# A hybrid decoder layer in fp32: head 3 projected by stored weight units, and the last head's output rows ahead of its decays

## The chip, the cores and the metric

The kernel is one program on **one core** of a Trainium2 chip. The metric is the device time of one execution in microseconds; three executions of the kernel before took 2317.92, 2318.16 and 2319.36 us, median **2318.16 us**. The engines of the core are called by their names in the profile: PE (TensorE: matrix products; PEld is its loading of weights), DVE (VectorE), ACT (ScalarE), POOL (GpSimd) and SP (SyncE, which here issues nearly all transfers).

## The reference

One decoder layer on x of 1024 tokens x 1024 features, all in float32:

```python
x = x + 0.5 * swiglu(rms_norm(x, ffn1_norm), w_gate1, w_up1, w_down1)      # d_ff = 2816
x = x + hybrid_mixer(rms_norm(x, mix_norm), w_in, ..., w_out)
x = x + 0.5 * swiglu(rms_norm(x, ffn2_norm), w_gate2, w_up2, w_down2)
return rms_norm(x, final_norm)

def hybrid_mixer(h, ...):
    proj = h @ w_in            # q, k, v, z of 8 GDN heads x 128; gates b, a; z, x, B, C, dt of 16 SSM heads x 64
    q, k, v = silu(causal_dwconv(gdn_qkv, gdn_conv_w))
    o = gated_delta_rule(q, k, v, g, beta)                                  # chunked: a triangular solve per chunk
    o_gdn = rms_norm(o, gdn_norm_w) * silu(gdn_z)
    y = ssd_scan(...)          # Mamba-2, then gated by silu(ssm_z), rms_norm in two groups
    return concat([o_gdn, o_ssm]) @ w_out
```

The gated delta rule of one head: with the decays g and the step sizes beta, the products k kᵀ of each block give a lower triangular system; its inverse is applied to v and k, and a state of 128 x 128 is carried through the 8 blocks of 128 tokens.

## The kernel before, in words

**Products.** Every float32 operand of a large product is split into a rounded part (hi) and the rest (lo); ScalarE makes hi by a cast (L241) and VectorE lo by a subtraction (L242). TensorE then runs three products, hi·hi, hi·lo and lo·hi (`mm3`, L121 to L125). The two feed-forward parts and part of the projection into the mixer use Strassen's scheme, 7 products of half-sized operands in place of 8. In the gate and up phase these are L334 to L336; after each product a hook `prep` prepares operands of a coming one. ScalarE's SiLU of the gate is L380, its read-outs of PSUM are L343.

**Weight units.** The mixer projects q, k, v and z of its 8 GDN heads from the same normed tokens. `NESTED` is the number of heads (0, 1, 2, 3) that are projected directly, by `proj_half`: 2 column pairs x 2 columns x 2 halves x 8 blocks x 3 products. Heads 4 to 7 go by Strassen in two *chunks* each (chunk 2i holds k and q of a head, chunk 2i + 1 v and z). A chunk has 7 *units*: a combination of blocks of W_in, split into hi and lo. The units are made long before they are used, in the first feed-forward part, by the generator `win_units`: each `next` of it makes one unit, by one or two casts (tile `wunit`), at times a sum or difference (tile `wsum`) and two stores to `wu_scr` in DRAM. The raw columns (`wraw`) are loaded at the start of a chunk. `UP_CHUNKS` = 6 chunks are made in the gate and up phase, driven by `prep` in each step i, and the other 2 in the down phase, driven by `Down.prep`, which is called once for each block of w_down. In the mixer `chunk` loads a chunk's units back (4 slots), and L1259 to L1261 multiply them with token combinations.

**A GDN head.** For each of its 8 heads the mixer's loop
- loads the cumulated decays and takes two exponentials (`qe`, L1361, and `dt`, L1364, with a triangular mask on GpSimd between them);
- projects and convolves q, k, v and gates z (`qt`, `kt`, `vt_`, `zc`);
- runs the key part `k_part`: 8 transposes of `kt` (L1345), their squares' sums (`jd`, L1349) and the decayed keys `kd` (L1350);
- forms the products k kᵀ and k qᵀ (L1426, L1427), and solves the triangular systems: a substitution of 31 steps on VectorE (L1476, L1478), an exchange through DRAM (`fs_x`), then small products on TensorE (from L1496 on);
- carries the state through 8 blocks, norms the result (`sso`, `co`, `vr`, L1567) and stores it to `mix_scr`.

The solve and the state chain of a head run while TensorE does the projection of the next head. The last head (7) has no next one; in its place stand the first output rows: `out_start` loads 256 rows of W_out (x) and the scanned SSM output (y), makes w (hi, lo) and mtt (hi by L1200, lo by L1201), and `group_tile(0, …)` forms the first 4 row blocks x 2 halves of the output (`FIRST_TILES`), read out of PSUM by L1220 into `xa`. `group_prep(1)` does the same for the next 256 rows.

**Order.** Each engine takes its instructions in its own fixed order. A scheduler sets it when the program is built, from the order of the code, the free buffers and pins (`tc.issue_after`). The code of the last head before:

```python
copy = chunk(pre[:, 3:3 + L], zc)                 # L1397: the units of v and z
    A.activation(out=kt, in_=kt, func=AF.Silu)    # L1399
tk, br2, kd = k_part(h, kt)                       # L1400
    A.activation(out=qt, in_=qt, func=AF.Silu)    # L1402
if h == GH - 1:
    out_start()                                   # L1404
conv_from(pre, 16 + h, vt_)
A.activation(out=zc, in_=zc, func=AF.Silu)
A.activation(out=vt_, in_=vt_, func=AF.Silu)
```

with `group_prep(1)` and the 8 calls of `group_tile(0, …)` behind it, and the two exponentials at the head of the loop.

Of the kernel before, what the change touches and what calls it, by code (L numbers as in the profile page):

```python
# [11 lines left out]
F32 = mybir.dt.float32  # L12
# [9 lines left out]
P = 128  # L22
# [22 lines left out]
def kernel(  # L45
# [28 lines left out]
    wu_scr = [dram.tile([P, 7, 2, 512], F32, name=f"wu_scr{i}") for i in range(2 * (GH - 4))]  # L74
# [279 lines left out]
    def gate_up_all(pool, H, w_gate, w_up, scr, raws, ops, last, work, tail, side):  # L354
# [66 lines left out]
        for i, (p, w) in enumerate(todo):  # L421
# [7 lines left out]
            def prep(grp):  # L429

                if nxt:
                    made = a_ops(pool, *((raws[0], m, nxt[0]) for m in A_GROUPS[grp]))
                    if i == 2 and grp == 0:
                        first_hid(made)
                    with ExitStack() as pins:
                        if i == 4 and grp == 0:
                            for e in made:
                                pins.enter_context(tc.issue_after(e.ins))
                        for _ in range(0 if i < 4 else 2 if grp and i % 3 == 1 else 1):
                            next(side, None)  # L440
                elif tail:
                    tail.pop(0)()
                if raws and grp == 1:
                    next_load()
# [57 lines left out]
    class Down:  # L502
# [25 lines left out]
        def prep(self):  # L528
            if self.cnt % 2:
                next(self.side, None)  # L530
# [109 lines left out]
    for h in range(4):  # L640
        w_seq.append((COL_Q + h * P, COL_K + h * P))
        w_seq.append((COL_V + h * P, COL_GZ + h * P))
# [11 lines left out]
    NESTED, UP_CHUNKS = 4, 6  # L654
# [556 lines left out]
    def group_tile(n, b, dh, w, m):  # L1211
        bs = slice(b * P, (b + 1) * P)
        ds = slice(dh * 512, (dh + 1) * 512)
        p = psum("pj")
        for j in range(2):
            last = mm3(p, m[0][:, j, bs], m[1][:, j, bs], w[0][:, j, ds], w[1][:, j, ds], j == 0, j == 1)
        o = out_bufs[0][b // 2][:, b % 2, ds]
        r = rstd_g[n // 2][:, b:b + 1]
        if n == 0:
            A.mul(out=o, in_=p, mul=r)  # L1220
        else:
            V.scalar_tensor_tensor(out=o, in0=p, scalar=r, in1=o, op0=ALU.mult, op1=ALU.add)
        return last

    FIRST_TILES = 4
    out_bufs, ready0 = [], []

    def out_start():
# [8 lines left out]
        for j in range(2):  # L1237
            split(w[0][:, j], w[1][:, j], x[:, j])
            ssm_split(0, j, y, *m)
# [93 lines left out]
    with ExitStack() as cg:  # L1333
        g1 = cg.enter_context(tc.tile_pool(name="gdn1", bufs=1, reuse_waits="tile"))
        g2 = cg.enter_context(tc.tile_pool(name="gdn2", bufs=2, reuse_waits="tile"))
        def k_part(h, kt):
# [4 lines left out]
            for half in range(2):  # L1341
# [4 lines left out]
                for i in range(4):  # L1346
# [3 lines left out]
                    A.mul(out=kd[:, b], in_=pt[:, i * P:(i + 1) * P], mul=wend[:, b, h:h + 1])  # L1350
# [5 lines left out]
        for h in range(GH):  # L1356
            hl = h % 2
# [5 lines left out]
            for b in range(NB):  # L1363
                A.activation(out=dt[:, b], in_=dt[:, b], func=AF.Exp, bias=ngc[:, b, h:h + 1])  # L1364
            qt = gp.tile([P, L], F32, name="qt", tag="xst", bufs=2)
            kt = g2.tile([P, L], F32, name="kt", bufs=3)
            vt_ = g1.tile([P, L], F32, name="vt_")
            if h < NESTED:
# [3 lines left out]
                tk, br2, kd = k_part(h, kt)  # L1372
# [15 lines left out]
            else:  # L1388
# [11 lines left out]
                tk, br2, kd = k_part(h, kt)  # L1400
                with tc.issue_after(copy.ins):
                    A.activation(out=qt, in_=qt, func=AF.Silu)  # L1402
                if h == GH - 1:
                    out_start()  # L1404
                conv_from(pre, 16 + h, vt_)
                A.activation(out=zc, in_=zc, func=AF.Silu)
                A.activation(out=vt_, in_=vt_, func=AF.Silu)
            nc.sync.dma_start(out=z_scr[h], in_=zc)
            if h == GH - 1:
                ready1 = group_prep(1)  # L1410
                for b in range(FIRST_TILES):
                    for dh in range(2):
                        tile_end = group_tile(0, b, dh, *ready0[0])
# [6 lines left out]
            for b0 in range(0, NB, 2):  # L1420
# [8 lines left out]
                for i in range(2):  # L1429
# [5 lines left out]
                                in1=dt[:, b2], op=ALU.mult)  # L1435
            fs_u = dram.tile([4, NB, 32, 32], F32, name="fs_u", bufs=2)
# [301 lines left out]
```

## Time and profile before

| | |
|---|---|
| median of 3 executions | 2318.16 us (2317.92 to 2319.36) |
| the profiled execution's own time | 2318.03 us |
| its span in the profile | 2316.3 us |
| mean granted clock of TensorE | 0.993 |
| instructions | 31,987 |
| read from DRAM, written | 249.34 MB, 105.52 MB |

The profile's views that are read below: the **page** has busy time of each engine and the *chain that ended last*, which follows the work back from the last instruction through what released each step. The **waits** of an engine list line, releaser, and then us in total, number and the longest. The **stretches** give for a window A:B (us from the start of the span) its length, the busy time of each engine with the number of instructions, the granted clock of TensorE (PEclk, 1.00 is full speed), the share of time in which the DMA engines moved something, and GB/s. In the **timeline** a row has the time at which the instruction starts, its duration, engine, line and operation, out<-in, the size, and in brackets a wait ahead of it; rows of the same kind that follow one another are folded (x8) with the sum of their durations. **Groups** (line, engine, operation) have busy time and mean ns of one, then the idle time ahead of them and what ended it. **Transfers** have KB each and us from issue to landing.

### The profile page before, as it was taken

What the parts mean: (1) busy time and instruction counts of PE and PEld (TensorE: products, weight loads), DVE (VectorE), ACT (ScalarE), POOL (GpSimd) and SP (SyncE); (2) the same over time, 40 slices, a digit from 0 to 9 for tenths busy, and PEclk for the clock granted to TensorE, in tenths of its full rate; (3) what the DMA queues carried; (4) which work ended last, traced back from release to release, by engine and by line L of the source; (5) the groups of instructions that cost most, each with busy time, mean ns of one, the idle gap of its engine ahead of it and who ended that gap; (6) DMA issues with size and microseconds to landing.
All of it is one profiled execution on the core that took longest, in us unless ns stands there. A gap on an engine that the chain in (4) does not pass through costs nothing.

```text
span 2316.3 us, 31987 instructions
## 1 busy us (share of the span) xinstructions
PE 2267.1 (98%) x11654; PEld 1848.9 (80%) x11654; DVE 1753.3 (76%) x3217; ACT 1179.7 (51%) x2284; POOL 50.6 (2%) x117
## 2 busy tenths in 40 slices
PE   7999999999999999999999998999999999999998
PEld 5788888888878878877877776888878888888886
DVE  8998987769777787656667778578698777766787
ACT  7444433354367985874655557432443333334344
POOL 0000000000000110000000000000000000000000
PEclk9999999999999999999999999899999999999999
DMA  3467663496653343242356556335223333329445
GB/s 111 159 210 241 228 207 115 170 334 214 210 187 125 128 128 98 69 128 65 83 165 180 168 172 216 103 98 191 91 72 119 109 106 109 104 89 357 138 154 214
DMA packets 262194, 356.96 MB, mean 154 GB/s; under 512 B 60808, under 2 KB 167404, under 8 KB 260244
## 3 DMA queue, kind: packets, MB, share of 16 engines
q1 hardware_dynamic: 261364, 352.73, 46.7%
q8 instruction: 91, 1.49, 0.3%
q0 software_dynamic: 672, 2.19, 0.2%
q14 instruction: 67, 0.55, 0.1%
HBM read 249.34 MB, written 105.52 MB: 153 GB/s over the span
## 4 chain that ended last, share of the span: by engine, by line
PE 79%; DVE 9%; ACT 7%; DMA 2%; issue 2%; POOL 0%; SPq 0%; DVEq 0%; ACTq 0%; POOLq 0%
PE ps_pj L124 6%; PE ps_pj L123 6%; PE ps_pj L125 6%; PE ps_pj L334 6%; PE ps_pj L335 6%; PE ps_pj L336 6%; PE ps_mx L334 3%; PE ps_mx L336 3%; PE ps_mx L335 3%; PE ps_pj L564 2%; PE ps_pj L565 2%; PE ps_pj L563 2%; PE ps_pj L1259 2%; PE ps_pj L1261 2%; PE ps_pj L1260 2%
## 5 line engine op out<-in xcount | busy, mean ns | idle before, releaser
L336 PE MATMUL ps_pj<-bh,al 128*128 128x512 f32 x688 | 267.9, 389 | 0.0
L335 PE MATMUL ps_pj<-bl,ah 128*128 128x512 f32 x688 | 267.8, 389 | 0.0
L334 PE MATMUL ps_pj<-bh,ah 128*128 128x512 f32 x688 | 267.5, 390 | 0.0
L125 PE MATMUL ps_pj<-hhi,wlo 128*128 128x512 f32 x576 | 229.9, 399 | 0.0
L123 PE MATMUL ps_pj<-hhi,whi 128*128 128x512 f32 x576 | 229.4, 398 | 0.4 <-ACT gsb L901 0.4
L124 PE MATMUL ps_pj<-hlo,whi 128*128 128x512 f32 x576 | 228.9, 397 | 0.0
L335 PEld LDWEIGHTS ps_pj<-bl,ah 128*128 128x128 f32 x688 | 129.2, 188 | 26.7
L336 PEld LDWEIGHTS ps_pj<-bh,al 128*128 128x128 f32 x688 | 129.2, 188 | 26.7
L334 PEld LDWEIGHTS ps_pj<-bh,ah 128*128 128x128 f32 x688 | 129.0, 188 | 26.6
L242 DVE TENSOR_TENSOR al<-as,ah 128x512 fp32r<-128x512 f32 x220 | 141.1, 685 | 7.3 <-ACT ah L241 6.8
L317 DVE TENSOR_TENSOR as<-wst 128x512 f32<-128x512 f32 x220 | 144.3, 684 | 2.5 <-DMA wst<-in_ffn_w_up_dram 2.4
L241 ACT CAST ah<-wst 128x512 fp32r<-128x512 f32 x88 | 54.5, 621 | 179.1 <-PE ps_oo L335 116.7
L241 ACT CAST hid<-hraw 128x1024 fp32r<-128x1024 f32 (+1 forms) x84 | 82.2, 980 | 123.6 <-PE ps_oo L565 45.6
L334 PE MATMUL ps_mx<-bh,ah 128*128 128x512 f32 x352 | 139.3, 398 | 5.2 <-ACT sg L380 2.1
L335 PE MATMUL ps_mx<-bl,ah 128*128 128x512 f32 x352 | 139.0, 395 | 0.4 <-DVE bl L242 0.4
L336 PE MATMUL ps_mx<-bh,al 128*128 128x512 f32 x352 | 138.2, 393 | 1.0 <-DVE al L242 1.0
L241 ACT CAST ah<-as 128x512 fp32r<-128x512 f32 x220 | 125.2, 617 | 19.6 <-DVE as L317 19.5
L123 PEld LDWEIGHTS ps_pj<-hhi,whi 128*128 128x128 f32 x576 | 108.4, 188 | 21.6 <-ACT gsb L901 0.9
L124 PEld LDWEIGHTS ps_pj<-hlo,whi 128*128 128x128 f32 x576 | 108.4, 188 | 21.4 <-issue 0.8
L125 PEld LDWEIGHTS ps_pj<-hhi,wlo 128*128 128x128 f32 x576 | 108.3, 188 | 20.9 <-issue 0.5
L242 DVE TENSOR_TENSOR hid<-hraw,hid 128x1024 fp32r<-128x1024 f32 (+1 forms) x84 | 95.0, 1131 | 26.6 <-ACT hid L241 26.3
L343 ACT COPY m<-ps_pj 128x512 f32<-128x512 f32 x88 | 51.6, 588 | 112.9 <-PE ps_pj L336 112.7
(502 smaller groups left out, 5651.6 us busy)
## 6 DMA issues: line engine op xcount, KB each, us to landing
hraw<-hid_scr SPq DMA_DIRECT2D x70, 512.0 KB, 4.3
wu_scr<-wunit SPq DMA_DIRECT2D x112, 256.0 KB, 3.2
wunits<-wu_scr SPq DMA_DIRECT2D x56, 512.0 KB, 4.7
hid_scr<-hs SPq DMA_DIRECT2D x110, 256.0 KB, 3.0
wst<-in_ffn_w_down_dram SPq DMA_DIRECT2D x50, 512.0 KB, 4.7
wst<-in_ffn_w_gate_dram SPq DMA_DIRECT2D x22, 1024.0 KB, 5.6
wst<-in_ffn_w_up_dram SPq DMA_DIRECT2D x22, 1024.0 KB, 5.5
hid_scr<-sg SPq DMA_DIRECT2D x44, 256.0 KB, 2.0
```

Source lines behind the costliest of these rows:

```text
L123: T.matmul(o, lhsT=wh, rhs=mh, start=first, stop=False)
L124: T.matmul(o, lhsT=wh, rhs=ml, start=False, stop=False)
L125: return T.matmul(o, lhsT=wl, rhs=mh, start=False, stop=last)
L241: return (A.copy(out=hi, in_=src), V.tensor_tensor(out=lo, in0=src, in1=hi.bitcast(F32), op=ALU.subtract))
L242: V.tensor_tensor(out=lo, in0=src, in1=hi.bitcast(F32), op=ALU.subtract))
L317: V.tensor_tensor(out=t, in0=v[0], in1=v[1], op=v[2])
L334: T.matmul(bank, lhsT=wh[:, k], rhs=bh[:, k], start=a, stop=False, skip_group_check=True)
L335: T.matmul(bank, lhsT=wh[:, k], rhs=bl[:, k], start=False, stop=False, skip_group_check=True)
L336: T.matmul(bank, lhsT=wl[:, k], rhs=bh[:, k], start=False, stop=z, skip_group_check=True)
L343: A.copy(out=t, in_=bank)
L563: T.matmul(bank, lhsT=hh, rhs=wh, start=first and k == 0, stop=False, skip_group_check=True)
L564: T.matmul(bank, lhsT=hh, rhs=wl, start=False, stop=False, skip_group_check=True)
```

## The change

The number of directly projected heads goes from 4 to 3 (`NESTED`), so head 3 is projected by units like heads 4 to 7. There are then 10 chunks of units instead of 8: 7 are made in the gate and up phase and 3 in the down phase. In the gate and up phase the first units still come at step i = 4; from there on each first `prep` of a step makes one unit and each second one two (before: two in every third step). In step 4 the units of both are pinned behind the operands that the `prep` makes (before: of the first alone). In the down phase three of five calls make a unit (before: every second).

In the mixer the key part of a directly projected head moves behind its z. In the last head, `out_start` makes both halves of mtt ahead of the splits of w, the 8 calls of `group_tile(0, …)` stand ahead of the key part and of the decays (now a function, `decays`), the decayed keys are made by VectorE, the convolution of v and the SiLUs of z and v come behind them, z is stored from GpSimd's queue, and `group_prep(1)` stands behind the products k kᵀ, pinned behind the sixth read-out of the output rows (`moved[5]`).

```diff
@@ -71,7 +71,7 @@
     g_scr = dram.tile([NG, L], F32, name="g_scr")
-    wu_scr = [dram.tile([P, 7, 2, 512], F32, name=f"wu_scr{i}") for i in range(2 * (GH - 4))]
+    wu_scr = [dram.tile([P, 7, 2, 512], F32, name=f"wu_scr{i}") for i in range(2 * (GH - 3))]
     t_scr = {m: dram.tile([P, 2, 4, 512], F32, name=f"t_scr{m}") for m in (4, 5, 6, 7)}
@@ -433,10 +433,10 @@
                     with ExitStack() as pins:
-                        if i == 4 and grp == 0:
+                        if i == 4:
                             for e in made:
                                 pins.enter_context(tc.issue_after(e.ins))
-                        for _ in range(0 if i < 4 else 2 if grp and i % 3 == 1 else 1):
+                        for _ in range(0 if i < 4 else 1 + grp):
                             next(side, None)
@@ -526,7 +526,7 @@
         def prep(self):
-            if self.cnt % 2:
+            if self.cnt % 5 not in (0, 3):
                 next(self.side, None)
@@ -637,7 +637,7 @@
         w_seq.append((COL_SZ + un * 256, None))
-    for h in range(4):
+    for h in range(3):
         w_seq.append((COL_Q + h * P, COL_K + h * P))
@@ -651,7 +651,7 @@
 
-    NESTED, UP_CHUNKS = 4, 6
+    NESTED, UP_CHUNKS = 3, 7
     IN_ORDER = (1, 6, 2, 5, 7, 3, 4)
@@ -1217,13 +1217,13 @@
         if n == 0:
-            A.mul(out=o, in_=p, mul=r)
+            moved.append(A.mul(out=o, in_=p, mul=r))
         else:
 ...
     FIRST_TILES = 4
-    out_bufs, ready0 = [], []
+    out_bufs, ready0, moved = [], [], []
 
@@ -1235,8 +1235,9 @@
         for j in range(2):
+            ssm_split(0, j, y, *m)
+        for j in range(2):
             split(w[0][:, j], w[1][:, j], x[:, j])
-            ssm_split(0, j, y, *m)
         ready0.append((w, m))
@@ -1347,14 +1348,18 @@
                     A.activation(out=jd, in_=pt[:, i * P:(i + 1) * P], func=AF.Square, accum_out=tk[:, b:b + 1])
-                    A.mul(out=kd[:, b], in_=pt[:, i * P:(i + 1) * P], mul=wend[:, b, h:h + 1])
+                    if h == GH - 1:
+                        V.tensor_scalar(out=kd[:, b], in0=pt[:, i * P:(i + 1) * P],
+                                        scalar1=wend[:, b, h:h + 1], scalar2=None, op0=ALU.mult)
+                    else:
+                        A.mul(out=kd[:, b], in_=pt[:, i * P:(i + 1) * P], mul=wend[:, b, h:h + 1])
             V.tensor_scalar(out=tk, in0=tk, scalar1=EPS, scalar2=None, op0=ALU.add)
 ...
 
-        for h in range(GH):
-            hl = h % 2
+        def decays(h):
+
             qe = g2.tile([P, L], F32, name="qe")
@@ -1362,6 +1367,12 @@
                 A.activation(out=dt[:, b], in_=dt[:, b], func=AF.Exp, bias=ngc[:, b, h:h + 1])
+            return qe, dt
+
+        for h in range(GH):
+            hl = h % 2
+            if h < GH - 1:
+                qe, dt = decays(h)
             qt = gp.tile([P, L], F32, name="qt", tag="xst", bufs=2)
@@ -1369,7 +1380,6 @@
                 conv_silu(g1, wa, 1, cw_g, 8 + h, kt)
-                tk, br2, kd = k_part(h, kt)
                 wa = next_w()
@@ -1397,20 +1407,27 @@
                     A.activation(out=kt, in_=kt, func=AF.Silu)
-                tk, br2, kd = k_part(h, kt)
+                if h < GH - 1:
+                    tk, br2, kd = k_part(h, kt)
                 with tc.issue_after(copy.ins):
                     A.activation(out=qt, in_=qt, func=AF.Silu)
-                if h == GH - 1:
+                if h < GH - 1:
+                    conv_from(pre, 16 + h, vt_)
+                    A.activation(out=zc, in_=zc, func=AF.Silu)
+                    A.activation(out=vt_, in_=vt_, func=AF.Silu)
+                else:
                     out_start()
-                conv_from(pre, 16 + h, vt_)
-                A.activation(out=zc, in_=zc, func=AF.Silu)
-                A.activation(out=vt_, in_=vt_, func=AF.Silu)
-            nc.sync.dma_start(out=z_scr[h], in_=zc)
-            if h == GH - 1:
-                ready1 = group_prep(1)
-                for b in range(FIRST_TILES):
-                    for dh in range(2):
-                        tile_end = group_tile(0, b, dh, *ready0[0])
+                    for b in range(FIRST_TILES):
+                        for dh in range(2):
+                            tile_end = group_tile(0, b, dh, *ready0[0])
+                    tk, br2, kd = k_part(h, kt)
+                    qe, dt = decays(h)
+                    conv_from(pre, 16 + h, vt_)
+                    A.activation(out=zc, in_=zc, func=AF.Silu)
+                    A.activation(out=vt_, in_=vt_, func=AF.Silu)
+            (G if h == GH - 1 else nc.sync).dma_start(out=z_scr[h], in_=zc)
+            if h < NESTED:
+                tk, br2, kd = k_part(h, kt)
 
@@ -1433,6 +1450,9 @@
                                 in1=dt[:, b2], op=ALU.mult)
+            if h == GH - 1:
+                with tc.issue_after(moved[5].ins):
+                    ready1 = group_prep(1)
             fs_u = dram.tile([4, NB, 32, 32], F32, name="fs_u", bufs=2)
```

How this moves instructions is shown at three places.

On **ScalarE**, in the first step of the gate phase, before the change (`wst` are raw weights as loaded, `ah` and `bh` rounded parts for the gate's own products, `wraw` and `wunit` belong to the weight units, `sg` is the SiLU of the gate read from PSUM):

```order
L343 COPY m_744<-ps_oo 128x512
L241 CAST bh_651<-bs 128x512 x2
L241 CAST ah<-wst 128x512
L241 CAST wunit<-wraw 128x512
L241 CAST ah<-as 128x512
L380 ACT_TABLE_LOAD
L380 ACTIVATE sg_759<-ps_pj 128x512
L380 ACTIVATE sg_760<-ps_mx 128x512
```

and after it:

```order
L343 COPY m_746<-ps_oo 128x512
L241 CAST bh_653<-bs 128x512 x2
L241 CAST ah<-wst 128x512
L241 CAST ah<-as 128x512
L380 ACT_TABLE_LOAD
L380 ACTIVATE sg_761<-ps_pj 128x512
L380 ACTIVATE sg_762<-ps_mx 128x512
```

The cast of the first unit, which stood ahead of the SiLU, is gone from here; it comes later in the phase.

On **ScalarE**, in the last head, before (`kt`, `qt`, `dt`, `qe`, `kd` as above, `vr` the result of head 6, `y`, `cols`, `mtt`, `x` and `w` the operands of the first output rows):

```order
L1399 ACTIVATE kt<-kt 128x1024
L1402 ACTIVATE qt<-qt 128x1024
L1200 ACTIVATE mtt<-y_13586,cols 128x1024
L1567 ACTIVATE vr<-vr,co 128x128 x8
L1361 ACT_TABLE_LOAD
L1361 ACTIVATE qe<-dt 128x1024
L241 CAST w_13589<-x_13585 128x1024 x2
L1364 ACTIVATE dt<-dt,ngc 128x128 x8
L1349 ACTIVATE jd,tk<-ps_mx 128x128
L1350 ACTIVATE kd<-ps_mx,wend 128x128
```

and after (the lines are numbered anew: L1366 and L1369 are the exponentials, L1576, L1582 and L1587 the result of head 6, L1413 the SiLU of q):

```order
L1413 ACTIVATE qt<-qt 128x1024
L1576 COPY vr<-ps_oo 128x128
L1200 ACTIVATE mtt<-y_13608,cols 128x1024
L1582 ACTIVATE jk_12681,sso<-vr 128x128
L1200 ACTIVATE mtt<-y_13608,cols 128x1024
L1366 ACT_TABLE_LOAD
L1366 ACTIVATE qe<-dt 128x1024
L241 CAST w_13611<-x_13607 128x1024 x2
L1369 ACTIVATE dt<-dt,ngc 128x128 x3
L1587 ACTIVATE vr<-vr,co 128x128 x8
L1369 ACTIVATE dt<-dt,ngc 128x128 x5
L1220 ACTIVATE xa<-ps_pj,rg_7266 128x512 x2
```

Both halves of mtt now stand ahead of the exponentials (before, the second one stood behind the key part, below the rows shown), and the first read-outs of the output rows stand ahead of the key part.

On **TensorE**, in the same place, before (L1259 to L1261 are the last units of v and z, `w` and `mtt` the output rows):

```order
L1259 MATMUL ps_pj<-t_10851,wunits 128x512
L1260 MATMUL ps_pj<-t_10853,wunits 128x512
L1261 MATMUL ps_pj<-t_10851,wunits 128x512
L1345 MATMUL ps_mx<-ident,kt 128x128 x8
L123 MATMUL ps_pj<-w_13589,mtt 128x512
L124 MATMUL ps_pj<-w_13590,mtt 128x512
L125 MATMUL ps_pj<-w_13589,mtt 128x512
```

and after, where L1260 to L1262 are the units:

```order
L1260 MATMUL ps_pj<-t_10206,wunits 128x512
L1261 MATMUL ps_pj<-t_10208,wunits 128x512
L1262 MATMUL ps_pj<-t_10206,wunits 128x512
L123 MATMUL ps_pj<-w_13611,mtt 128x512
L124 MATMUL ps_pj<-w_13612,mtt 128x512
L125 MATMUL ps_pj<-w_13611,mtt 128x512
L123 MATMUL ps_pj<-w_13611,mtt 128x512 x2
```

The 8 transposes of the keys, which stood between the units and the output rows, now come behind 48 products of output rows; 18 more of these follow, and then the small products of the solve of head 6 (L1516, before L1496, which stood behind the transposes and 20 products).

## The prediction

> **What bounds the kernel now.** I read the page first: TensorE is the bound, and the chain that ended last runs on it for four fifths of the span.
>
> ```profile
> span 2316.3 us, 31987 instructions
> PE 2267.1 (98%) x11654; PEld 1848.9 (80%) x11654; DVE 1753.3 (76%) x3217; ACT 1179.7 (51%) x2284; POOL 50.6 (2%) x117
> PE 79%; DVE 9%; ACT 7%; DMA 2%; issue 2%; POOL 0%; SPq 0%; DVEq 0%; ACTq 0%; POOLq 0%
> ```
>
> So a gain comes from three things only: fewer matmuls, fewer stretches in which TensorE waits, fewer in which its clock is cut. Next I read TensorE's own waits (line, what ended the wait, us in total, times, longest).
>
> ```profile
> PE ps_pj L123 <- ACT xa L1220: 4.9, 2, 4.7
> PE ps_pj L123 <- ACT mtt L1200: 2.9, 1, 2.9
> PE ps_mx L1426 <- ACT kd L1350: 2.5, 3, 1.4
> PE ps_mx L334 <- ACT sg L380: 2.1, 1, 2.1
> PE ps_mx L1345 <- ACT kt L862: 1.8, 2, 1.6
> PE ps_pj L125 <- DVE mtt L1201: 0.7, 1, 0.7
> PE ps_pj L124 <- DVE w L242: 0.6, 1, 0.6
> ```
>
> Four of these seven (L1220, L1200, L1201, L242) stand in one place, the first output rows in the last head: 4.7 + 2.9 + 0.7 + 0.6 = 8.9 us. Third, the busy time in stretches cut where the granted clock (PEclk) changes.
>
> ```profile
> core 0: us, PE busy (x) PEld busy (x) DVE busy (x) ACT busy (x) POOL busy (x), PEclk, DMA share, GB/s
> 70.64:74.05 3.41, 1.28 (x7) 0.74 (x5) 1.47 (x3) 3.38 (x6) 0.00 (x0) 1.00 0.27 94
> 74.05:77.46 3.41, 3.41 (x8) 2.73 (x9) 2.93 (x5) 2.05 (x4) 0.00 (x0) 0.50 0.00 0
> 1179.47:1182.88 3.41, 1.79 (x13) 1.64 (x13) 0.00 (x0) 3.40 (x10) 0.00 (x0) 1.00 0.98 313
> 1432.56:1435.97 3.41, 0.96 (x3) 0.48 (x3) 2.48 (x11) 3.39 (x9) 0.00 (x0) 1.00 0.26 39
> 1435.97:1439.38 3.41, 2.93 (x6) 1.82 (x6) 3.41 (x6) 3.40 (x4) 0.00 (x0) 0.50 0.31 48
> 1439.38:1442.80 3.42, 0.00 (x0) 0.00 (x0) 3.42 (x4) 3.21 (x4) 0.00 (x0) 1.00 0.57 183
> 1442.80:1446.21 3.41, 2.34 (x35) 1.55 (x35) 2.46 (x5) 3.21 (x7) 0.00 (x0) 0.50 0.84 265
> 1446.21:1459.86 13.65, 13.65 (x99) 10.24 (x100) 4.30 (x6) 6.13 (x9) 0.00 (x0) 0.50 0.27 94
> ```
>
> After a stretch of 3.41 us in which TensorE was busy 1.28, 0.96 or 0.00 us the clock was 0.50; after one with 1.79 us it stayed 1.00. At half clock TensorE does half its work, so the last head loses (2.93 + 2.34 + 13.65) / 2 = 9.5 us to the clock, and with the waits **18.4 us**. The first gate step loses 2.1 + 3.41 / 2 = **3.8 us**.
>
> **The change, part by part.** The sum is made against the profiled execution, 2318.03 us (1.7 outside its span); the median of the three runs, 2318.16, is the same within their spread.
>
> *Head 3 by units: minus 5.6 us.* Projected directly it takes 2 column pairs x 2 columns x 2 halves x 8 blocks x 3 = 192 matmuls; as two chunks 2 x 7 x 4 x 3 = 168. The other matmuls keep their number. The last 50 unit matmuls of the last head give the pace:
>
> ```profile
> 1416.07 0.48 PE L1260 MATMUL ps_pj<-hlo,wunits 128*128 128x512 f32 x1
> 1427.41 0.39 PE L1261 MATMUL ps_pj<-t,wunits 128*128 128x512 f32 x1
> ```
>
> (1427.41 - 1416.07) / 49 = 0.231 us from start to start, and 24 x 0.231 = 5.6. The mean of 389 ns that the page gives overlaps its neighbours and would make it 9.3; I don't use it.
>
> *Later start of the units: minus 3.8.* ScalarE takes its work in order, and in the first gate step a unit's cast stood in the queue before its weights had landed:
>
> ```profile
> 66.39 0.62 ACT L241 CAST ah<-wst 128x512 fp32r<-128x512 f32 x1
> 70.45 0.62 ACT L241 CAST wunit<-wraw 128x512 fp32r<-128x512 f32 x1 [3.44 <-DMA wraw<-in_w_in_dram]
> 71.61 1.28 ACT L380 ACT_TABLE_LOAD   x1
> 72.91 0.60 ACT L380 ACTIVATE sg<-ps_pj 128x512 f32<-128x512 f32 x1
> ```
>
> That wait of 3.44 us made the reads of PSUM at L380 late, on which TensorE waited its 2.1 us, and the clock fell. The new order has no unit there, and the weights are asked for as early as before. Bounds: 0 if VectorE, which had two subtractions of units here and is the next to be late, keeps TensorE waiting just as long; 3.8 if it does not. The nearest row is the wait of 3.44 us itself, longer than the 2.1 that goes, so I take all of it.
>
> *The keys' transposes behind v and z in the direct heads: minus 2.6.* The 1.6 us at L1345 is head 3, which no longer has a direct projection to stand behind; it goes. Of the 2.5 us at L1426, where the products of k wait for the casts of kd, I take 1.0, between 0 and 2.5.
>
> *The last head: minus 10.9.* Before, ScalarE and VectorE did the following between the end of the last state product of the head before (1415.90, I call it E) and the first product of its solve, L1496:
>
> ```profile
> 1419.34 1.14 ACT L1200 ACTIVATE mtt<-y,cols 128x1024 fp32r<-128x1024 f32 x1
> 1420.38 2.44 ACT L1567 ACTIVATE vr<-vr,co 128x128 f32<-128x128 f32 x8
> 1425.09 1.98 ACT L241 CAST w<-x 128x1024 fp32r<-128x1024 f32 x2
> 1433.32 1.23 ACT L1200 ACTIVATE mtt<-y,cols 128x1024 fp32r<-128x1024 f32 x1
> 1443.10 1.82 ACT L1220 ACTIVATE xa<-ps_pj,rg 128x512 f32<-128x512 f32 x3
> 1431.73 0.17 DVE L1478 TENSOR_TENSOR fx<-fx,ft 128x8 f32<-128x8 f32 x1
> 1434.90 1.28 DVE L1201 SCALAR_TENSOR_TENSOR mtt<-y,cols,mtt 128x1024 fp32r<-128x1024 f32 x1
> 1444.60 0.44 DVE L1490 STREAM_TRANSPOSE lv<-lv 128x256 f32<-128x256 f32 x1
> 1445.10 0.25 PE L1496 MATMUL ps_sc<-lv,u 32*32 32x32 f32 x1
> ```
>
> The second half of mtt came at 1433 to 1436, behind the key part, and the first results left PSUM (xa) only at 1443. In the new order both halves of mtt stand ahead of the exponentials. Set in a row with these durations: E + 3.9 both halves on ScalarE, + 5.2 the table, + 6.2 qe, + 8.2 both casts of w; on VectorE mtt's low halves by + 6.0, w's by + 10.9 and + 13.1. TensorE has 42 units left at E (8 fewer than before) and ends them at + 9.7; it waits **1.0** for w, then runs 48 output products, 8 transposes and 18 more products to + 27.1. There the solve is due. Its steps on VectorE end at + 16.7 (before + 15.9), the exchange through DRAM and VectorE's queue took 13.0 us before (1431.73 to 1444.60), and 12.5 of it again gives + 29.2: a wait of **2.1**. Behind it the moved key part (kd on VectorE, one step of ScalarE and one of VectorE by turns, with wlo between them) holds xa and the solve's copies by **2.5**. Waits 5.6; bounds 1.0 (only w) and 10 (the solve 4 us later). The clock: a gap of 2.1 us falls wholly into one stretch of 3.41 us in 4 cases of 10, so I add 2.0 and have 7.6 left of 18.4. The store of z on POOL's queue is hidden unless it lands after E + 28.7, since ScalarE's qsq reuses its buffer; it starts near + 18, and the slowest transfer of twice its size on that queue took 9.5 us:
>
> ```profile
> x<-in_w_out_dram POOLq DMA_DIRECT2D x1, 1024.0 KB, 9.5
> ```
>
> The Trainium skill, in "TensorE: Matmul & The Clock Gate", Part 1, has the clock drop after at least one idle window of about 3.4 us and return after one busy window. By that the 2.1 us would be harmless and the sum 2.0 lower; this trace differs, with a drop after a stretch 1.28 us busy, and 13.65 us at half clock in which TensorE was never idle.
>
> *Two more chunks of units: plus 0.5.* Each has 7 subtractions and 4 sums on VectorE:
>
> ```profile
> L242 DVE TENSOR_TENSOR wunit<-wsum,wunit 128x512 fp32r<-128x512 f32 x32 | 21.6, 686 | 1.2 <-DMA wu_scr<-wunit 0.6 <-ACT wunit L241 0.5
> L675 DVE TENSOR_TENSOR wsum<-wraw 128x512 f32<-128x512 f32 x16 | 11.0, 688 | 2.1 <-DMA wraw<-in_w_in_dram 1.9
> 200.00:250.00 50.00, 50.00 (x222) 41.42 (x221) 47.36 (x78) 25.53 (x47) 0.00 (x0) 1.00 0.62 216
> 560.00:590.00 30.00, 30.00 (x134) 24.85 (x133) 28.01 (x31) 13.50 (x16) 0.00 (x0) 1.00 0.42 137
> 590.00:600.00 10.00, 10.00 (x46) 8.29 (x45) 6.26 (x7) 3.13 (x5) 0.00 (x0) 1.00 0.74 230
> ```
>
> 11 x 0.69 = 7.5 us each, so 15 in all, beside 360 us in the up phase and 190 in the down phase. VectorE is at 95% and 93% in the fullest stretches, and TensorE never waits there. Bounds: 0 (the row of 590 to 600, 63%), and 7.5 in the down phase if all 11 fall where VectorE has no gap. I stay near the lower, since the new ones are spread over two products of six steps.
>
> **Sum:** 2318.0 - 5.6 - 3.8 - 2.6 - 10.9 + 0.5 = **2295.6 us**, 1.0% faster.
>
> **Rivals.** *The clock falls again in the last head.* The waits stay at 5.6 but the cold stretch lasts as long as before, 9.5: only 3.3 are saved there, **2303**. For it: the 13.65 us row. Against it: no wait of the new order reaches 2.9 or 4.7.
> *The rows fill the whole gap.* Waits of 1.0, no cold stretch: 17.4 saved, **2289**. Against it: TensorE arrives at the solve before the exchange can be done.
> *VectorE becomes the bound in the down phase.* Plus 7.5 in place of 0.5: **2303**.
> *The rows don't come earlier.* x still lands too late, the last head keeps its 18.4, and only units and starts gain: 2318.0 - 5.6 - 3.8 - 2.6 + 0.5 = **2306.5**.
> *Slower: the clock stays low.* A wait at the solve starts a cold stretch that small products can't end. Each us of it costs 0.5; with the last head's waits at 5.6 and the other gains kept it has to last 49 us to eat the 24.4 us that are then gained, and 70 us of it give **2329**. The longest on record is 17 us.
>
> **How the numbers follow.** Forecast (2291 to 2300) 0.42, clock again 0.20, gap filled 0.18, VectorE 0.08, rows late 0.07, slower 0.04, nothing measurable 0.01. The range takes in the first five, with the bounds of the unknown terms: 2285 to 2309. A difference of 0.2% (4.6 us) is about what a measurement of this kernel can tell from none: faster 0.94, same 0.02, slower 0.04.
>
> **What would show it.** In the profile after: 24 fewer matmuls at TensorE; no wait at L380 and clock 1.00 near 74 us; waits for xa and mtt gone, one of about 2 us before the solve of the last but one head; no clock of 0.50 near 1430, or one stretch of it. I am wrong if TensorE waits for units in head 3, for hid or wd in the down phase (from 440 us on), or if the last head waits over 10 us.

## The result and the profile after

The changed kernel took **2303.22 us** (median of 4 runs, 2300.86 to 2304.97) against 2318.04 us (4 runs, 2313.91 to 2319.36): a ratio of **0.9937, 95% interval 0.9923 to 0.9952**. It is 0.6% faster where 1.0% was forecast: 14.8 us in place of 22.5. The profiled execution took 2304.59 us.

The page, its first lines:

```profile
span 2302.9 us, 32052 instructions
PE 2256.3 (98%) x11630; PEld 1841.5 (80%) x11630; DVE 1764.3 (77%) x3253; ACT 1177.9 (51%) x2279; POOL 52.6 (2%) x115
```

TensorE has 24 matmuls less, and its busy time fell by 10.8 us. The rest of the span, in which it stood still, fell only from 49.2 to 46.6. Its waits say where (us in total, times, longest; rows that are nearly the same before and after are left out):

```profile
PE ps_pj L1260 <- DVE pre L1270: 4.0, 1, 4.0
PE ps_mx L1443 <- ACT kd L1355: 2.0, 2, 1.6
PE ps_sc L1516 <- DVE lv L1510: 1.6, 2, 1.5
PE ps_pj L564 <- DVE wd L242: 1.2, 3, 0.6
PE ps_pj L124 <- DVE w L242: 1.2, 1, 1.2
PE ps_oo L1565 <- ACT vn L1561: 0.9, 2, 0.5
PE ps_mx L334 <- ACT sg L380: 0.8, 1, 0.8
PE ps_sc L563 <- ACT hid L241: 0.8, 1, 0.8
PE ps_sc L1559 <- DVE rr L1556: 0.6, 1, 0.6
PE ps_pj L123 <- ACT xa L1220: 0.3, 1, 0.3
```

The waits for xa and mtt are gone and L380 costs 0.8 us in place of 2.1. But the largest wait of the mixer is **new**: 4.0 us at L1260, a unit product that waits until VectorE has read an earlier unit product out of PSUM (L1270) and so freed its place there, a bank. It stands in head 3, the head that the change projects by units. The stretches around it and in the last head, cut where the granted clock changes:

```profile
core 0: us, PE busy (x) PEld busy (x) DVE busy (x) ACT busy (x) POOL busy (x), PEclk, DMA share, GB/s
70.64:74.05 3.41, 2.59 (x12) 1.80 (x11) 2.22 (x5) 3.25 (x5) 0.00 (x0) 1.00 0.28 70
74.05:77.46 3.41, 3.41 (x16) 2.81 (x15) 3.32 (x6) 1.73 (x3) 0.00 (x0) 1.00 0.00 0
1170.28:1173.70 3.42, 1.48 (x7) 0.90 (x5) 3.42 (x6) 0.00 (x0) 0.00 (x0) 1.00 0.51 151
1173.70:1177.11 3.41, 1.30 (x6) 1.08 (x7) 3.41 (x9) 2.97 (x4) 0.00 (x0) 1.00 0.40 161
1177.11:1180.52 3.41, 3.41 (x10) 2.65 (x9) 2.54 (x8) 1.02 (x1) 0.30 (x1) 0.50 0.00 0
1443.35:1446.76 3.41, 1.78 (x40) 1.55 (x40) 3.35 (x6) 3.36 (x10) 0.00 (x0) 1.00 0.74 255
1446.76:1457.00 10.24, 10.23 (x80) 7.02 (x81) 3.58 (x10) 5.63 (x15) 0.00 (x0) 0.50 0.35 122
```

In the first gate step TensorE is busy and the clock stays at 1.00. In head 3 VectorE is busy through both stretches (3.42 and 3.41 us) while TensorE waits, and the clock is halved behind them. In the last head the clock falls again, behind the wait for the solve (L1516). At half clock the two stretches cost (3.41 + 10.23) / 2 = 6.8 us; before it was 1.7 + 9.5 = 11.2.

### The profile page after: what moved, and what is told of

Read it like the earlier page. It is cut to its first block, busy times and chain, and to the rows that moved or that the text cites. A ratio compares the mean times of both kernels' runs of the same rounds, so it can differ in the third digit from the quotient of the medians.

```text
span 2302.9 us, 32052 instructions
## 1 busy us (share of the span) xinstructions
PE 2256.3 (98%) x11630; PEld 1841.5 (80%) x11630; DVE 1764.3 (77%) x3253; ACT 1177.9 (51%) x2279; POOL 52.6 (2%) x115
## 3 DMA queue, kind: packets, MB, share of 16 engines
q8 instruction: 91, 1.49, 0.3%
## 5 line engine op out<-in xcount | busy, mean ns | idle before, releaser
L123 PE MATMUL ps_pj<-hhi,whi 128*128 128x512 f32 x512 | 203.5, 398 | 0.4 <-ACT gsb L901 0.4
L125 PE MATMUL ps_pj<-hhi,wlo 128*128 128x512 f32 x512 | 203.8, 398 | 0.0
L124 PE MATMUL ps_pj<-hlo,whi 128*128 128x512 f32 x512 | 202.7, 396 | 0.0
L123 PEld LDWEIGHTS ps_pj<-hhi,whi 128*128 128x128 f32 x512 | 96.3, 188 | 19.7 <-ACT gsb L901 0.8
L125 PEld LDWEIGHTS ps_pj<-hhi,wlo 128*128 128x128 f32 x512 | 96.3, 188 | 19.4 <-issue 0.5
L124 PEld LDWEIGHTS ps_pj<-hlo,whi 128*128 128x128 f32 x512 | 96.3, 188 | 19.2 <-issue 0.8
```

The lines of the kernel that those rows point to most:

```text
L123: T.matmul(o, lhsT=wh, rhs=mh, start=first, stop=False)
L124: T.matmul(o, lhsT=wh, rhs=ml, start=False, stop=False)
L125: return T.matmul(o, lhsT=wl, rhs=mh, start=False, stop=last)
```

## Experiments

All times are medians beside runs of the kernel before on the same chip, with the ratio to those and its 95% interval. The ratio can differ from the quotient of the two medians by up to 0.0006, some 1.4 us, so a difference between two runs is given by the ratios, and by the medians too where these say something else. L numbers are of the kernel named; the edits move some by a line or two.

**The changed kernel again**, beside the next three.

> The changed kernel itself, timed again beside the other three so that they can be compared with it on one chip. Expected: 2301 to 2305 us, with the two marks of the first profile: a wait of 4 us of TensorE for the read-out of a unit product in head 3, and a stretch at half clock of 10 us or less behind the solve in the last head. If the second mark hangs on where the throttle's windows happen to fall, it differs from profile to profile while the first one stays.

Measured 2304.12 us (5 runs, 2300.78 to 2308.28); ratio 0.9944, 0.9931 to 0.9958. In its profile the wait in head 3 is 3.91 us, with 6.83 us at half clock behind it, and the last head, which waits its 1.47 us again, has **no** stretch at half clock:

```profile
1170.03:1173.45 3.42, 0.13 (x1) 0.00 (x0) 3.42 (x7) 1.29 (x2) 0.00 (x0) 1.00 0.91 297
1173.45:1180.27 6.82, 6.20 (x15) 4.83 (x16) 4.89 (x11) 2.69 (x3) 0.30 (x1) 0.50 0.01 5
1443.10:1446.51 3.41, 2.66 (x45) 2.02 (x45) 3.05 (x7) 3.36 (x8) 0.00 (x0) 1.00 0.88 316
```

So the first mark stays, and the second depends on where the throttle's stretches fall. The five runs had mean clocks of 0.994 to 0.996; the longest, 2308.28 us, had the lowest.

**The key part of head 2 early.** First theory: the change had moved the key part too far back, so that VectorE was late.

```diff
                 conv_silu(g1, wa, 1, cw_g, 8 + h, kt)
+                if h == NESTED - 1:
+                    tk, br2, kd = k_part(h, kt)
...
-            if h < NESTED:
+            if h < NESTED - 1:
                 tk, br2, kd = k_part(h, kt)
```

> Only the key part of head 2 goes back ahead of its v and z. Theory A (the key part came late, so head 2's products of k, its substitution and head 3's first chunks fall on VectorE together): the wait of 4.05 us at L1260 goes below 0.5 us, no clock of 0.50 in head 3, and the first unit starts behind the first product of k of head 2 and not 6.8 us ahead of it; 2.5 to 5.7 us less than the changed kernel, the lower end if the wait of 1.6 us for the silu of kt comes back. Rival B (units crowd VectorE in whichever head comes first by units): the wait stays at 3 to 4 us and the time within 1.5 us of the changed kernel.

Measured **2319.99 us**, ratio 1.0006 (0.9997 to 1.0014): the whole gain was gone. The waits of its TensorE:

```profile
PE ps_pj L1260 <- DVE pre L1270: 21.7, 5, 5.2
```

The wait did not go; it came in every head by units, five times, up to 5.2 us. Both theories had missed this. What the edit moved was the order that the scheduler gives VectorE in all of these heads (the table further down counts it), and that is where the next theory came from.

**Head 3 direct again**, with all the rest of the change.

```diff
-    for h in range(3):
+    for h in range(4):
...
-    NESTED, UP_CHUNKS = 3, 7
+    NESTED, UP_CHUNKS = 4, 6
```

> Head 3 is projected directly again (8 chunks of units, 6 of them in the gate and up phase), all else as changed. TensorE has 24 matmuls more. Theory A (the units of head 3 saved 5.6 us and gave 5.7 back, 4.05 of waiting and 1.7 of half clock): within 2 us of the changed kernel. Rival B (the units bring their 5.6 us and the shortfall lies elsewhere): 4 to 7 us more than the changed kernel.

Measured **2299.82 us**, ratio 0.9917 (0.9905 to 0.9930), beside 0.9944 (0.9931 to 0.9958) for the changed kernel on the same chip: with 24 matmuls more it is 4.3 us *faster*. By the ratios the difference is 6.3 us. Rival B is out, and theory A's "within 2 us" was wrong too: it set 5.7 us of loss against 5.6 of gain, and the loss is larger. The profile has no wait of 0.3 us or more for the read-out of a unit product; in the last head it waits 1.95 us for xa and not for the solve. The mean clocks of its runs are 0.997 to 0.999, where the changed kernel had 0.994 to 0.996.

**The last head in the old order**, five heads by units kept.

```diff
+            qe, dt = decays(h)
...
+                tk, br2, kd = k_part(h, kt)
...
+                if h == GH - 1:
                     out_start()
...
+                conv_from(pre, 16 + h, vt_)
...
+            if h == GH - 1:
+                ready1 = group_prep(1)
+                for b in range(FIRST_TILES):
```

> The last head in the old order (decays and key part first, decayed keys by ScalarE, old place of the splits and of the second rows, z from the old queue), all else as changed. Theory A (the first output rows ahead of the key part save 18.4 - 8.1 = 10.3 us there): 8 to 12 us more than the changed kernel, waits for mtt and xa of 7 to 9 us and 15 us or more at half clock are back. Rival C (most of it was where the throttle's windows fell): under 5 us more.

Measured 2316.06 us, ratio 0.9990 (0.9981 to 0.9998): 11.9 us more than the changed kernel (10.7 by the ratios), as theory A said. The wait that is back is larger than it was:

```profile
PE ps_pj L123 <- ACT xa L1220: 11.1, 2, 10.8
```

with 23.9 us at half clock behind 1436.5 us. The last head's new order carries most of the gain of the change, 10.7 of 13.0 us by the ratios.

**Why TensorE waits in head 3.** The timeline of VectorE in the changed kernel's head 3 shows what stands ahead of the read-out (L1270) for which TensorE waits from 1171.76 to 1175.81. L847 is a tap of the convolutions of keys and queries, L1496 and L1498 are a step of the substitution of head 2:

```profile
1167.95 0.21 DVE L1496 TENSOR_TENSOR ft<-fx,fu 128x49 f32<-128x49 f32 x1
1168.19 0.21 DVE L1498 TENSOR_TENSOR fx<-fx,ft 128x49 f32<-128x49 f32 x1
1168.44 0.20 DVE L1496 TENSOR_TENSOR ft<-fx,fu 128x42 f32<-128x42 f32 x1
1168.56 1.28 DVE L847 SCALAR_TENSOR_TENSOR kt<-pre,cols,kt 128x1024 f32<-128x1024 f32 x1
1169.76 0.20 DVE L1498 TENSOR_TENSOR fx<-fx,ft 128x42 f32<-128x42 f32 x1
1169.88 1.28 DVE L847 SCALAR_TENSOR_TENSOR kt<-pre,cols,kt 128x1024 f32<-128x1024 f32 x1
...
1171.18 1.28 DVE L847 SCALAR_TENSOR_TENSOR qt<-pre,cols,qt 128x1024 f32<-128x1024 f32 x1
...
1172.48 1.28 DVE L847 SCALAR_TENSOR_TENSOR kt<-pre,cols,kt 128x1024 f32<-128x1024 f32 x1
...
1173.78 1.28 DVE L847 SCALAR_TENSOR_TENSOR qt<-pre,cols,qt 128x1024 f32<-128x1024 f32 x1
1174.97 0.18 DVE L1498 TENSOR_TENSOR fx<-fx,ft 128x28 f32<-128x28 f32 x1
1175.07 0.69 DVE L1270 TENSOR_TENSOR pre<-ps_pj,zc 128x512 f32<-128x512 f32 x1
```

VectorE never pauses; the read-out is late because five taps, 1.2 us apart, stand directly ahead of it, and 11 pairs of substitution steps, 0.5 us each, ahead of the taps (3 more pairs stand between them). Theory E: the wait is the sum of what VectorE's order puts between this read-out and the one before. Two experiments change that sum.

**The decays of head 3 behind its convolutions**, which lets ScalarE start them earlier.

```diff
-            if h < GH - 1:
+            if h < GH - 1 and h != NESTED:
                 qe, dt = decays(h)
...
                 conv_from(pre_q, h, qt)
+                if h == NESTED:
+                    qe, dt = decays(h)
```

> The changed kernel with the two exponentials of head 3 placed behind the convolutions of its keys and queries, no other edit. In VectorE's order the six taps of these convolutions (L847, 1.28 us each) then stand behind 6 pairs of substitution steps and not behind 11, so 8 pairs come between them and the next read-outs of unit products. Theory E (TensorE's wait in head 3 is the place of the six taps in VectorE's order, directly ahead of the read-out that frees the bank): the wait of 3.9 to 4.05 us goes below 1 us, no half clock in head 3, 4 to 7 us less than the changed kernel. Rival D (VectorE has too much work in that stretch in any order): 3 us or more of waiting for a read-out stay in head 3, within 1.5 us of the changed kernel.

Measured 2299.26 us, ratio 0.9923 (0.9909 to 0.9937), where the changed kernel had 0.9944 (0.9931 to 0.9958). The wait is 2.70 us, between the two expectations, and 6.83 us at half clock stay behind it: "below 1 us" and "no half clock" were wrong. The time is 4.9 us less by the ratios, as theory E had it, but the intervals overlap, and a wait that is 1.35 us shorter doesn't explain it: the edit moved other waits too (that for kd in head 4 is gone, xa and kd in the last head have 1.5 and 1.1 us).

**Three taps of head 3's queries left out**, so that only the term made by ScalarE is left of that convolution.

```diff
-                conv_from(pre_q, h, qt)
+                if h == NESTED:
+                    A.mul(out=qt, in_=pre_q[:, 3:3 + L], mul=cw_g[:, 3, h:h + 1])
+                else:
+                    conv_from(pre_q, h, qt)
```

> The changed kernel without the three taps of the convolution of head 3's queries (left out: three of the four terms of that convolution). In VectorE's order the same 11 pairs of substitution steps stand ahead of the keys' taps, and three steps of 1.28 us are gone between them and the read-out that frees TensorE's bank. Theory E (TensorE waits in head 3 for VectorE's queue, each us of VectorE ahead of that read-out is a us of waiting): the wait of 3.9 to 4.05 us falls by 3 x 1.28 = 3.8, to 0.3 us or less, and with it the half clock in head 3; 4 to 7 us less than the changed kernel. Rival F (the substitution itself, which waits for the exchange or for ScalarE, sets the read-out): the wait stays above 2.5 us.

Measured 2297.18 us, ratio 0.9902 (0.9889 to 0.9915). The wait is 1.49 us, again between the two, and no half clock follows it. The expectation had counted wrong: of the three taps only two stand ahead of the read-out (see the timeline above; the third comes after it). That 4.05 - 2 x 1.28 gives just 1.49 is partly chance, since a tap takes 1.20 us from start to start and one pair went as well. The time, 9.7 us less by the ratios and 6.9 by the medians, fell by more than the wait and the half clock behind it had cost (2.6 of 4.05 us, and 1.7 to 3.1); here too other waits moved (a new one of 1.9 us at L1260 in the last head, none above 0.6 us for kd), and what makes up the rest was not tried.

Counted in VectorE's order, from the read-out before to the awaited one (s is a pair of substitution steps, counted where its second step stands, K and Q a tap of keys and queries, R a read-out of a unit product), with the sum of 0.50 us a pair and 1.20 us a tap set against the first row:

```
kernel, head                          VectorE's order                pairs taps  wait by the sum  measured
changed, 3                            R s11 K s1 KQ s1 KQ s1 R         14    5        -             4.05
key part of head 2 early, 3           R s12 KQ s1 KQKQ R               13    6       4.75           4.66
key part of head 2 early, 4 to 6      R s13 KQ s1 KQKQ R               14    6       5.25       5.10 to 5.20
decays of head 3 late, 3              R s6 KK s1 KQ s1 QQ s1 R          9    6       2.75           2.70
queries' taps left out, 3             R s11 K s1 KK s1 R               13    3       1.15           1.49
key part of head 2 early, 7           R s7 KK s1 KQ s1 Q R              9    5       1.55           1.58
```

The sum meets all the waits within 0.35 us; it was made after the runs, whose own forecasts had missed. It can hold because TensorE's side is the same in all rows: its wait begins 9.3 to 9.5 us behind the first R, after 40 or 41 unit products. VectorE takes 12.6 us from R to R in the changed kernel's head 3. In its heads 4 to 7 a read-out stands between the taps, VectorE takes 3.8 to 9.2 us from one to the next, and nothing waits. So theory E stands: TensorE waits for VectorE's *order*, not for its load. The next run tests that with the same load in another order.

**The key part of all three direct heads early**, as in the kernel before.

```diff
                 conv_silu(g1, wa, 1, cw_g, 8 + h, kt)
+                if True:
+                    tk, br2, kd = k_part(h, kt)
...
-            if h < NESTED:
+            if False:
                 tk, br2, kd = k_part(h, kt)
```

> The changed kernel with the key part of all three direct heads back ahead of v and z. In VectorE's order read-outs of unit products of head 3 then stand between the taps. Theory E: no wait of 3 us or more for a read-out in any head; the waits for kd and kt of the direct heads come back, about 2 to 4 us, so between 3 us less and 1 us more than the changed kernel. Rival D: waits for read-outs of 4 us or more, as in the run with head 2's key part alone, and 2310 us or more.

Measured 2300.59 us, ratio 0.9931 (0.9919 to 0.9944). VectorE's order in head 3 is R s2 K s1 R K s1 K s9 Q R s1 Q R s1 Q R, and the waits of 950 to 1450 us are:

```profile
PE ps_pj L123 <- ACT xa L1220: 2.8, 2, 2.0
PE ps_mx L1445 <- ACT kd L1355: 2.7, 3, 1.5
PE ps_pj L1260 <- DMA wunits<-wu_scr: 2.1, 1, 2.1
PE ps_mx L1346 <- ACT kt L862: 0.4, 2, 0.2
PE ps_pj L1260 <- DVE pre L1270: 0.3, 1, 0.3
PE ps_sc L1518 <- DVE lv L1512: 0.2, 1, 0.2
```

The wait in head 3 is 0.3 us with the same six taps. In return kd is waited for, and in the last head a load of units comes 2.1 us late and the output rows wait 2.8 us for xa, with 13.65 us at half clock behind; no theory had this. The same block put back for one head and for three heads gives ratios of 1.0006 and 0.9931, some 17 us apart. Rival D is out; against the changed kernel the time is 3.0 us less by the ratios (3.5 by the medians), at the edge of what theory E had, with intervals that overlap.

**The same edit with head 3 direct** prices the move of the key part by itself.

> Head 3 direct, and the key part of the four direct heads ahead of v and z as before the change, all else as changed. This is the price of the moved key part where no units follow: by the prediction's term 2.6 us more than the run with head 3 direct (waits of about 2.3 us for kd in head 0 and 1.6 us for kt in head 3 come back), by a rival within 1 us of it since the waits are taken later.

Measured 2300.59 us, ratio 0.9931 (0.9917 to 0.9945), against 0.9917 (0.9905 to 0.9930) with the key part late. The two lie 0.0014, some 3 us, apart, near the term's 2.6, though the intervals overlap. By the medians it is 0.8 us, so the term is supported and not measured. The waits came as expected: 2.5 us for kd and 1.8 us for kt are back; in the last head 1.4 us for kd came in place of the 2.2 for xa.

**Fewer units in the down phase**, head 3 direct.

```diff
-            if self.cnt % 5 not in (0, 3):
+            if self.cnt % 2:
```

> Head 3 direct, and in the down phase a unit in every second call as before the change and not in three of five. Price of the denser units in the down phase: in the run with head 3 direct TensorE waited 1.9 us for a cast of hid near 495 us and 0.9 us for wd, and its clock was at half for 3.41 us behind that. If the denser units are the cause: these waits go below 0.6 us and 2 to 4 us less than the run with head 3 direct, about 2297. If they come from elsewhere (the end of the up phase): the waits stay, and the time is within 1 us.

Measured 2297.46 us, ratio 0.9919 (0.9906 to 0.9933), which is no difference from 0.9917. The waits for hid (1.9 us) and wd (0.9) fell to nothing and 0.7, but one at the end of the phase, near 645 us, grew from 0.9 to 1.9 us. So the denser units cost nothing that can be measured.

**The start of the units alone**, on the kernel before.

```diff
-                        if i == 4 and grp == 0:
+                        if i == 4:
```

> The kernel before with one edit: in step 4 the units of both hooks, not of the first alone, are pinned behind the operands of the step, so that the first unit's cast leaves the first gate step. By the prediction's term 3.8 us less than before (2.1 of waiting for L380 and 1.7 of half clock); by its lower bound 0, if VectorE is next to be late there.

Measured 2314.91 us, ratio 0.9982 (0.9973 to 0.9991): 4.2 us by the ratio, from 2.1 to 6.3 (3.6 by the medians), where 3.8 was forecast. The wait for L380 is 0.8 us in the profile and the clock is 1.00 at 74 us.

**Five row blocks of first output rows**, in the changed kernel and with head 3 direct and the units of the down phase as before.

```diff
-    FIRST_TILES = 4
+    FIRST_TILES = 5
```

> The changed kernel with five row blocks of first output rows in place of four. If the wait of 1.47 us for the solve of head 6 starts the stretch at half clock behind it: 12 products x 0.231 = 2.8 us more stand ahead of the solve, the wait goes, and the half clock behind it too, 1.5 to 6 us less than the changed kernel. If something else starts it: the half clock of 6.8 us or more stays behind 1440 us, and the time is within 1.5 us.

Measured 2301.87 us, ratio 0.9925 (0.9913 to 0.9937). In the last head neither a wait for the solve nor a half clock is left; the stretch that holds the small products is now full:

```profile
1443.27:1446.69 3.42, 3.38 (x43) 2.22 (x42) 3.38 (x5) 3.37 (x9) 0.00 (x0) 1.00 0.83 296
```

One profile can't show by itself that the wait for the solve, with the sparse small products behind it, had started the stretch at half clock, since the second profile of the changed kernel had the wait and no half clock either. The count in the last section speaks for it: every drop of the clock came behind a stretch in which TensorE was busy for 52.2% or less, as it was from 1443.35 us (1.78 of 3.41 us). The gain is 4.4 us by the ratios and 2.2 by the medians, within what was expected, with intervals that overlap; 1.1 and 0.7 us of new waits came later (near 1585 and 1594 us).

> Head 3 direct, units in every second call of the down phase, and five row blocks of first output rows in place of four, so 12 products more stand ahead of the solve of head 6. Expected if the wait of 1.9 us for xa and the half clock behind it in the last head come from too little work of TensorE ahead of that place: the wait goes below 1 us, no half clock there, 2 to 4 us less than the run with four row blocks (2297.46), about 2294. If the read-outs of xa on ScalarE are what is late in any case: a wait of 1.5 us or more for xa stays, and the time is within 1.5 us of that run.

Measured **2297.47 us** (4 runs, 2296.79 to 2297.73), ratio **0.9906** (0.9892 to 0.9919). The longest wait for xa is 0.4 us where it was 1.96, without half clock in the last head. Whether the time follows is open: by the ratios it is 3.0 us less than the run with four row blocks, as expected, by the medians no less, and the intervals overlap. It is ahead of the kernel before and of the changed one, whose intervals are 0.9923 to 0.9952 and 0.9931 to 0.9958.

## Why the prediction was right or wrong

The time came within the range, but 7.6 us above the forecast and outside the band of 2291 to 2300. By its terms:

- **Head 3 by units, minus 5.6: the step that failed.** The matmuls did go: of the 10.8 us that TensorE's busy time fell, 11.2 - 6.8 = 4.4 are the clock, and 6.4 are left for 24 matmuls. But the term counted TensorE's products alone and said "The other matmuls keep their number" of the rest; the new unit products of head 3 were given no wait. The runs show a wait of 3.9 to 4.05 us there, and behind it half clock that cost 1.7 us in one profile (3.41 us of it) and 3.1 in the other (6.83 us with TensorE busy 6.2), set by VectorE's order in head 3, which the prediction had not read. Set against the run without them, the units of head 3 make the kernel 4.3 us slower by the medians (6.3 by the ratios), not 5.6 faster. The wait and the half clock are 5.7 to 7.0 us of that difference of 10 to 12; another 1.1 us for kd and 1.5 in the state chains (below) go with the units too. The prediction did name the mark ("if TensorE waits for units in head 3"), without a rival or a price for it.
- **Later start of the units, minus 3.8.** Right: alone it gave 4.2.
- **The keys' transposes, minus 2.6.** The waits for kd and kt, 2.5 + 1.8 us before, are 2.0 after, so 2.3 went; taken back with head 3 direct they cost about 3. But 1.6 of the 2.0 us now stand in head 4. That and 1.5 us of new waits in the state chains (for the small tiles vn and rr) are in the changed kernel, and none of them is above 0.4 us with head 3 direct; what in the order makes them was not tried.
- **The last head, minus 10.9.** 7.6 us of waits and clock were to stay; 1.25 + 1.47 + 0.27 of waits and 5.1 of clock, 8.1, stayed. The sum held by luck, by two errors: of the waits, 1.0 for w, 2.1 for the solve and 2.5 behind it, 1.25, 1.47 and 0.27 came, 3.0 in place of 5.6; and the clock, given 2.0, fell for 10.24 us. (18.4 - 7.6 is 10.8, and 1431.73 to 1444.60 is 12.9 and not 13.0; neither changes the sum by more than 0.1.) That a wait at the solve takes the clock with it 4 times in 10 can't be judged by two profiles: with the same wait of 1.47 us the clock fell in the first and not in the second. The reason given, a gap that falls wholly into one stretch, is not what decides: TensorE was busy 1.78 us in the stretch ahead of the fall and 2.66 us in the one of the second profile.
- **Two more chunks, plus 0.5.** Not contradicted: in the down phase 0.8 us of waits for hid in this profile, which the kernel before does not have, and 0.4 for wd as before; with head 3 direct, fewer units in that phase made no difference.

Of the rivals, "the clock falls again in the last head" gives 2303, the time measured, but with waits of 5.6 and a cold stretch of the old length; the place that cost the time was head 3, and that this rival met the number was luck. VectorE did become what TensorE waited for, in the mixer and not in the down phase. The parts taken singly, 10.7 for the last head, 4.2 for the start, 3.2 for the keys and -6.3 for head 3 by units, make 11.8 us by the ratios, near the 13.0 of the whole on the same scale.

## What to carry to other kernels

A rewrite that saves products on the bound engine changes the order of all that feeds it: read the other engines' order between two read-outs, add up what stands there, and set it against the time in which the bound engine fills its free banks, some 9.4 us here. In this kernel pairs of 0.5 us and taps of 1.2 us account for each wait once one is known. And where several edits come together, take each one out: this change gained 14.8 us with a headline part that cost 4 to 6.

## What the runs showed of the hardware

**The clock's rule is sharper than the prediction had it.** Counted in the 14 profiles in stretches of 3.413 us from one change of the clock to the next, 43 stretches at full clock were followed by half clock, and in all of them TensorE was busy 52.2% of the time or less. Of 9236 that were followed by full clock it was busy 52.4% or more in all but two; one of the two, at 43%, is the stretch from 1170.28 us of the changed kernel shown above, where the clock fell one stretch later; behind the other, at 49%, it did not fall. So some 1.6 us of waiting is enough if it falls within one stretch, and may be harmless when two stretches share it. The Trainium skill, in "TensorE: Matmul & The Clock Gate", Part 1, has at least one idle window before the drop; the stretch of 1443.35 us, 1.78 us busy, had none and was followed by it.

**A kernel's scatter is in part this clock.** The stretches begin at other places of the program in each execution, so that a wait hits or misses. In the first step of the second feed-forward part TensorE waits for the same two operands in all 14 profiles, 1.34 to 1.39 us and 0.54 to 0.55 us; behind it the clock fell for 3.41 us in 8 of them and not in the other 6. In the second profile of the changed kernel (first two rows) one stretch holds both waits; in its first profile (last two rows) two stretches share them:

```profile
1682.03:1685.45 3.42, 1.52 (x6) 0.78 (x6) 3.32 (x6) 1.42 (x3) 0.00 (x0) 1.00 1.02 337
1685.45:1688.86 3.41, 3.41 (x10) 2.63 (x9) 3.29 (x7) 2.21 (x4) 0.00 (x0) 0.50 0.79 259
1685.70:1689.11 3.41, 2.05 (x10) 1.39 (x8) 3.31 (x6) 1.86 (x3) 0.00 (x0) 1.00 0.65 175
1689.11:1692.52 3.41, 2.86 (x12) 2.01 (x13) 3.34 (x6) 1.43 (x3) 0.00 (x0) 1.00 1.09 359
```

Runs with head 3 direct lay from 2295.49 us at a mean clock of 0.999 to 2303.95 us at 0.997, of the changed kernel from 2300.78 at 0.996 to 2308.28 at 0.994. It is not the whole: the first four runs of the changed kernel, all at 0.996, lie 4.1 us apart. One profile of a kernel therefore says little on whether a cold stretch belongs to it: the profiles of the first set have the changed kernel at 2299.1 us and the one with head 3 direct at 2302.2, the reverse of their medians.
